# A hybrid encoder layer on one core: late low halves last in each product, a last row block in two tiles, and a new table of step times

## The chip, the cores and the metric

The kernel runs on one core of a Trainium2 chip. The core has five engines, each with a queue of its own that it works off in order: TensorE (PE; its weight loads are PEld), VectorE (DVE), ScalarE (ACT), GpSimd (POOL) and SyncE (SP), which here issues nearly all DMAs. The metric is the device time of one execution in microseconds (us).

## The reference

One layer of an encoder with two head groups side by side, for x of 1 × 4096 × 1024 in float32:

```python
def rmsnorm(x, g):
    y = xf * lax.rsqrt(jnp.mean(xf * xf, axis=-1, keepdims=True) + EPS)
    return y * g
...
#   x <- x + RMSNorm_post( W_out [ attn_out * silu(g_a) ; pool_out * silu(g_p) ] )
#   where [q | k | v | g_a | u_p | g_p] = RMSNorm_pre(x) @ W_in
#   - attention: windowed GQA (|i-j| <= 128) in blocks of 128 queries, 8 query and 2 key heads of 64,
#     a learned sink logit per head, T5 relative-position bias
#   - pooling: four channel groups, centred mean over windows 2/4/8/16 minus the token,
#     a linear map per group, a scale per channel
```

W_in has 1024 rows and 2304 columns, W_out is 1024 × 1024.

## The kernel before, in words

**Products.** TensorE works in fp16. Each float32 operand is a pair of a high and a low half (the low half is what the high one leaves), and each product is the sum of three terms: high by high, low weight by high x, high weight by low x. `high`/`low` (L2144, L2148), `x_hi`/`x_lo` (L336, L341) and lines 524 and 527 make the halves: ScalarE casts the high one, and VectorE or GpSimd subtracts it to get the low one. Before, the three terms alternate inside the loop over k, so that the third matmul of a product already reads the second low half.

**Phase one** (0 to about 484 us) computes the pooling half and the gates of RMSNorm_pre(x) @ W_in. The 4096 tokens are cut into eight macro-tiles m of 512. Macro-tile 0 uses plain products (`mm`, L975, `plain_ga`); the others use a scheme of seven products of half size (`product`, L1018) on sums of quarters of x and of the weights: A11, A12, S2, S1, S4, S3, A22. Meanwhile the weights are loaded (`w_load`, L395), multiplied by the norm's gain (`w_fold` on VectorE, L411; `w_fold_act` on ScalarE, L415), squared for their scale (`w_square`, L464; `norm_prod`, L468, sums the squares on TensorE), and written back to DRAM for phase two. The sums of squares of x's rows give row scales; `rs_row` (L306) stores the 512 of a macro-tile to DRAM in 4-byte pieces, and `rs_spread` (L310) loads them back as a broadcast `rb` for `y_scale` (L330). `x_turn` (L277) transposes the first x by DMA; `y_store` (L357) and `x_store` (L352, L354) keep x's halves in DRAM.

**Phase two** (about 484 us to the end) goes backward over 16 units u of two blocks of 128 rows, from block 31 to 0. For a block: `scores` (L1642), `logits` (L1659), `exps` (L1670), `probs` (L1713, high half) and `rests` (L1721, low half) make the probabilities `pn`, `turn` (L1733) transposes them by DMA, `values` (L2095) multiplies them with v, and `gate` (L2102) with the gate that `load_ga` (L2046) brings. `kv_product` (L1917) and `q_terms` (L1983) make k, v and q. The output product is again the scheme of seven (`product`, L2242), its sums are joined by `add` (L2284, tiles `mo`), and the norm follows: `square` (L2268), `mean` (L2294, L2299), `residual` (L2303), `store` (L2331). For the very last unit, 0, the output is four plain products per row block (`last_product`, L2214, with `last_square` L2229 and `last_gain` L2223), row block 1 in two tiles of 512 columns.

**Order.** Each step is put down by `due(t, fn, args)` with a time t from a plan written by hand; `moved` adds to that time what a table `later` (one per phase) holds for the step, sorts all steps by time, and the steps are issued in that order. Nothing is reordered after that: the numbers set only the order on each engine, not when something runs. SP's DMAs are in one queue too.

```python
out.append((t + later.get((*key, seen[key]), 0.0), n, fn, args))
```

## Time and profile before

| | |
|---|---|
| median of 3 executions | 1152.0 us (1149.72 to 1155.39) |
| the profiled execution | 1151.47 us |
| its span in the profile | 1149.6 us, mean granted clock 0.997 |
| TensorE busy | 1114.5 us (97%) |
| VectorE, ScalarE, GpSimd busy | 957.9 (83%), 723.3 (63%), 292.0 (25%) |
| moved by DMA | 262 MB, mean 228 GB/s |

In the rows of a timeline the first number is the start, the second the length (both us), then the engine, the line, what is written and what is read, a count, and in brackets the idle time before it and what ended that. A row of the waits names who waited for whom: us in total, times, the longest. SPq is SP's queue.

### The profile page before, as it was taken

Reading aid. Unit: us, or ns where it says so; the run is one execution under the profiler, and the core shown is the slowest. Engines: PE = TensorE matmul, PEld = TensorE weight load, DVE = VectorE, ACT = ScalarE, POOL = GpSimd, SP = SyncE. Lnnn points to the kernel's source line nnn. Section 1 sums busy time; section 2 is a strip of 40 time slices with the busy share of each in tenths; the row PEclk is TensorE's granted clock in tenths of the full one; section 3 lists DMA queues with packets and bytes.
Section 4 is the critical chain, followed back from the end, with each engine's and each line's share of the span. In section 5 each row is a group of like instructions: output and inputs, shape, how many; then the busy total and the mean of one; then the engine's idle time right before and its main releaser. Section 6 shows DMA issues by size and latency. Waiting matters only on the chain.

```text
span 1149.6 us, 28863 instructions
## 1 busy us (share of the span) xinstructions
PE 1114.5 (97%) x11532; PEld 816.6 (71%) x11532; DVE 957.9 (83%) x1973; ACT 723.3 (63%) x1622; POOL 292.0 (25%) x279
## 2 busy tenths in 40 slices
PE   6999999999999999999999999999999999999987
PEld 4547888888888888887566667667666666676443
DVE  6788787889869996867998898888888888988886
ACT  5766667666465635157766676676676666766672
POOL 1000000000000000001454554364454545544322
PEclk9999999999999999999999999999999999999999
DMA  9667878999879966999989898889989988889786
GB/s 250 169 230 247 229 214 303 265 266 275 268 231 279 262 238 215 346 266 256 251 193 214 210 211 208 211 187 239 208 186 227 197 198 223 211 206 200 141 186 199
DMA packets 328006, 262.02 MB, mean 228 GB/s; under 512 B 222608, under 2 KB 285712, under 8 KB 324416
## 3 DMA queue, kind: packets, MB, share of 16 engines
q1 hardware_dynamic: 323840, 245.50, 81.0%
q0 software_dynamic: 4032, 14.68, 5.2%
q8 instruction: 90, 1.47, 0.5%
q14 instruction: 44, 0.36, 0.1%
HBM read 130.87 MB, written 76.59 MB: 180 GB/s over the span
## 4 chain that ended last, share of the span: by engine, by line
PE 49%; DVE 26%; issue 9%; ACT 7%; DMA 6%; POOL 1%; SPq 0%; DVEq 0%; POOLq 0%; ACTq 0%
PE ch L1031 11%; PE aq_p L1983 7%; DVE p_all L1659 6%; DVE pn L1721 5%; PE ms L2242 5%; PE cl L1031 4%; PE m L2242 4%; PE a L981 4%; PE kp L1917 3%; PE pb L1031 3%; DVE ws L896 3%; DVE mo L2284 3%; PE pg L1092 2%; ACT pn L1713 2%; PE s L1642 1%
## 5 line engine op out<-in xcount | busy, mean ns | idle before, releaser
L1031 PEld LDWEIGHTS <-wa 128*128 128x128 f16 x3360 | 328.7, 98 | 38.9 <-issue 0.6
L1031 PE MATMUL ch<-xt,wa 128*128 128x256 f16 x1920 | 212.8, 273 | 0.3 <-ACT cbig L1043 0.3
L1670 ACT ACTIVATE p_all<-p_all,nm 128x385 f32<-128x385 f32 (+1 forms) x256 | 153.0, 599 | 59.0 <-DVE nm L1659 51.1
L1721 DVE SCALAR_TENSOR_TENSOR pn<-p_all,rd,pn 128x384 f16<-128x384 f32 (+1 forms) x256 | 159.0, 672 | 20.4 <-ACT pn L1713 18.6
L2242 PE MATMUL ms<-wa,ys 128*128 128x512 f16 x720 | 166.4, 381 | 3.9 <-DVE mo L2284 1.9
L1659 DVE CUSTOM_DVE_ANT_0 p_all<-s,ybig,nsink 128x385 f32<-128x385 f32 (+1 forms) x256 | 156.8, 664 | 7.9 <-PE s L1642 7.9
L1713 ACT ACTIVATE pn<-p_all,rd 128x384 f16<-128x384 f32 (+1 forms) x256 | 135.4, 596 | 8.9 <-issue 4.3
L2242 PE MATMUL m<-wa,y 128*128 128x512 f16 x540 | 124.2, 379 | 4.2 <-DVE mo L2284 3.3
L2242 PEld LDWEIGHTS <-ys 128*128 128x128 f16 x720 | 69.2, 98 | 81.7 <-issue 6.1
L1031 PE MATMUL cl<-xt,wa 128*128 128x256 f16 x960 | 106.3, 273 | 0.1
L2242 PEld LDWEIGHTS <-y 128*128 128x128 f16 x540 | 51.2, 98 | 65.4 <-issue 6.9
L249 POOL TENSOR_SCALAR ssq<-ssq 128x4 f32<-128x4 f32 (+1 forms) x11 | 3.7, 340 | 338.2 <-ACT jk L240 332.4
L2148 POOL TENSOR_TENSOR y<-yf,y 128x512 f16<-128x512 f32 x29 | 33.5, 1156 | 203.3 <-DMA wa<-w_scr 165.1
L341 DVE TENSOR_TENSOR xt<-ybig,xt 128x1024 f16<-128x1024 f32 x50 | 60.3, 1219 | 13.0 <-ACT xt L336 13.0
L2148 POOL TENSOR_TENSOR ys<-at,ys 128x512 f16<-128x512 f32 x28 | 36.5, 1305 | 132.1 <-ACT ys L2144 132.1
L2268 ACT ACTIVATE jkb<-mo 128x512 bf16<-128x512 f32 x42 | 26.3, 626 | 64.8 <-DVE mo L2284 64.8
L1917 PEld LDWEIGHTS <-raw 128*128 128x128 f16 x588 | 56.8, 98 | 14.1 <-issue 1.9
L1917 PE MATMUL kp<-xt,raw 128*128 128x256 f16 x540 | 65.4, 273 | 0.2 <-DVE at L2102 0.2
L2279 POOL TENSOR_TENSOR mo<-mo,ybig 128x512 f32<-128x512 f32 x39 | 52.4, 1343 | 45.2 <-ACT jkb L2268 45.0
L1642 PE MATMUL s<-k_all,q 64*32 64x288 f16 (+2 forms) x2856 | 60.0, 284 | 1.1 <-ACT k_all L1580 0.5
L1065 ACT ACTIVATE gp<-cbig,cg 128x256 f32<-128x256 f32 x42 | 19.0, 500 | 63.0 <-DVE cbig L1056 63.0
L336 ACT CAST xt<-ybig 128x1024 f16<-128x1024 f32 x50 | 51.6, 1040 | 7.2 <-PE cl L1031 4.4
(242 smaller groups left out, 2009.6 us busy)
## 6 DMA issues: line engine op xcount, KB each, us to landing
xn<-in_x SPq DMA_DIRECT2D x28, 512.0 KB
ybig<-in_xT SPq DMA_DIRECT2D x28, 512.0 KB
y_scr<-xt SPq DMA_DIRECT2D x14, 1024.0 KB
out<-mo SPq DMA_DIRECT2D x28, 512.0 KB
xt<-y_scr SPq DMA_DIRECT2D x26, 512.0 KB
xt<-in_x POOLq DMA_DIRECT2D x26, 512.0 KB, 5.0
xt<-x_scr SPq DMA_DIRECT2D x19, 512.0 KB
x_scr<-xt SPq DMA_DIRECT2D x9, 1024.0 KB
```

The source lines that it names most:

```text
L341: eng.tensor_tensor(out=o[:, w, 1], in0=y_view(i), in1=o[:, w, 0], op=ALU.subtract)
L1031: nc.tensor.matmul(acc[:, c], wa[:, q, wi, slot * HK + k, c * P : (c + 1) * P], x[:, xi, k, :], start=(fresh and n == 0), stop=(n > 3 * 2 ...
L1642: nc.tensor.matmul(s_bank[jj][r0 : r0 + nr, gg, lo:hi], q_t[u, half][a, qi, jj, tl + r0 : tl + r0 + nr], k_all[a, ki, k0 : k0 + hi - lo], ...
L1659: nc.vector.tensor_tensor_reduce(out=p_t[b, half][:, hh, :nk], in0=s_t[b, half][jj][:, gg, :nk], in1=bias[:, h, lo : lo + nk], scale=negc[ ...
L1670: nc.scalar.activation(p[:, hh, :nk], p[:, hh, :nk], AF.Exp, bias=nm_t[b, half][:, hh : hh + 1], scale=-1.0, accum_out=den_t[b, half][:, h ...
L1713: nc.scalar.activation(prob_view(b, half)[:, 0, i], p_t[b, half][:, i, :nk], AF.Copy, scale=rd_t[b, half][:, 0, i : i + 1],)
L1721: nc.vector.scalar_tensor_tensor(out=pn4[:, 1, i], in0=p_t[b, half][:, i, :nk], scalar=rd_t[b, half][:, 0, i : i + 1], in1=pn4[:, 0, i], o ...
L1917: nc.tensor.matmul(acc, wkv[:, slot, wi, k, :], x[:, xi, k, :], start=(onto is None and n == 0), stop=(n == 3 * HK - 1), skip_group_check= ...
L1983: nc.tensor.matmul(acc[:, jj], w[:, wi, jj, k, :], x[:, xi, k, :], start=(first and n == 0), stop=(last and n > 3 * 2 * HK - 3), skip_grou ...
L2148: eng.tensor_tensor(out=y[:, :, 1], in0=f(u), in1=y[:, :, 0], op=ALU.subtract)
L2242: nc.tensor.matmul(z_t[u, tag], y[:, k, yi, :], wo[o][:, wi, k // 2, k % 2, :], start=(n == 0 and acc is None), stop=(n == 3 * HK - 1), sk ...
L2279: eng.tensor_tensor(out=mo, in0=mo, in1=gpost[:, cs], op=ALU.mult)
```

## The change

It has three parts.

1. `term_order` puts the term with a late low half last: first, over all k, the high by high term and the one with the low half that is there early, then all matmuls with the other low half. It is used in `mm` (there the weight's low half is last), in both `product`s, `plain_ga`, `kv_product` and `last_product`. The number and shape of matmuls stay.
2. In unit 0, the second half of row block 1 is computed in two tiles of 256 columns, the second of them in a bank of the scores (`s_bank[1]`). `last_mean` adds what is known of the sum of squares ahead, `last_root` adds the rest, and the last 512 columns are finished by three engines: `residual` of 256 on VectorE, `last_rescale` of 256 on ScalarE and `last_sum` of these on GpSimd.
3. The two tables `later` get new entries and values. Three of them move the broadcasts `rs_spread` of macro-tiles 3, 5 and 6 (that of 4 gets a later time too).

```diff
+    def term_order(n, early=None):
+        a, b = ((0, 1), (1, 0)) if early else ((1, 0), (0, 1))
+        return [(k, w, x) for terms in (((0, 0), a), (b,)) for k in range(n) for w, x in terms]
...
-            for k in range(HK):
-                for wi, xi in ((0, 0), (1, 0), (0, 1)):
-                    for c in range(2):
+            for k, wi, xi in term_order(HK):
+                for c in range(2):
...
-            for k in range(KT):
-                for wi, xi in ((0, 0), (1, 0), (0, 1)):
+            for k, wi, xi in term_order(KT, "x"):
...
+            (x_turn, 0, 1): 0.4, ... (w_fold, 6, 1): -10.0, ... (rs_spread, 6, 1): 8.0, ...
+            (x_hi, 4, 'A11', 1): -10.0, ...
...
+    def last_mean():
+        ss = ss_t[0]
+        ms = rs_t["last"] = pb.tile([P, 1], F32, name="ms_last", tag="ms")
+        nc.vector.tensor_scalar(
+            out=ms, in0=ss[:, 2:3], scalar1=ss[:, 3:4], scalar2=epss, op0=ALU.add, op1=ALU.add
+        )
+
+    def last_root():
+        ms = pb.tile([P, 1], F32, name="ms_root", tag="ms")
+        nc.vector.tensor_tensor(out=ms, in0=ss_t[0][:, 4:5], in1=rs_t.pop("last"), op=ALU.add)
+        rs_t[0, 1] = pb.tile([P, 1], F32, name="rs_last", tag="rs")
+        nc.gpsimd.tensor_tensor(out=rs_t[0, 1], in0=ms, in1=mhalf, op=ALU.pow)
+
+    def last_rescale(cs):
+        mo = mo_t[0][1][:, cs]
+        nc.scalar.activation(mo, mo, AF.Copy, scale=rs_t[0, 1])
+
+    def last_sum(cs):
+        xr = xr_t[0][:, cs]
+        nc.gpsimd.tensor_tensor(out=xr, in0=mo_t[0][1][:, cs], in1=xr, op=ALU.add)
...
-    at_(36.8, last_product, 1, "22", O22, 1, True)
+    for part in QUARTERS:
+        at_(36.8, last_product, 1, "22", O22, 1, True, part)
...
-    at_(53.7, last_product, 1, "21", O12, 1, False)
+    at_(53.7, last_product, 1, "21", O12, 1, False, QUARTERS[0])
+    at_(55.0, last_product, 1, "21", O12, 1, False, QUARTERS[1])
...
+    at_(58.7, residual, 0, 1, LO)
+    at_(58.75, last_rescale, slice(768, D))
+    at_(58.8, last_sum, slice(768, D))
+    at_(59.4, residual, 0, 1, slice(512, 768))
...
+        ... (load_xr, 1, 1, 1): -0.8, (pool_in, 0, 0, 1): 1.5,
```

What that does to the queues, at three places. SP around 310 us, before; `rs_scr` is the store of the row scales of macro-tile 6, `rb6` their broadcast, `in_w_b` a weight of phase two:

```order
L306 DMA rs_scr_89<-ssq6_3302 128x4x1
L1107 DMA ga_scr_91<-sga4_1_1_3762 128x2x128 x2
L310 DMA rb6_3793<-rs_scr_89 128x512
L352 DMA x_scr_88<-xt_72 128x2048
L395 DMA raw_70<-in_w_b 128x1024
L1107 DMA ga_scr_91<-sga4_0_1_3854 128x2x128 x2
```

and in the changed kernel (its lines have other numbers):

```order
L311 DMA rs_scr_89<-ssq6_3302 128x4x1
L1109 DMA ga_scr_91<-sga4_1_1_3762 128x2x128 x2
L357 DMA x_scr_88<-xt_72 128x2048
L400 DMA raw_70<-in_w_b 128x1024
L1109 DMA ga_scr_91<-sga4_0_1_3852 128x2x128 x2
L315 DMA rb6_3884<-rs_scr_89 128x512
```

The broadcast has gone behind the store of x, the weight and two stores of gates. SP in the tail, before; `pn1_0` and `pn1_1` are the two transpositions of block 1, `ga_scr` the gate of block 1, `yp_scr` the pooled half (`pool_in`), `w_scr` the weights O12 of the last unit's products, `in_x` the x for the residual (`load_xr`):

```order
L1733 DMA_TRANSPOSE wa_73<-pn1_0_16154 128x24x128
L2046 DMA wa_73<-ga_scr_91 128x512
L2171 DMA yf0_0_16288<-yp_scr_90 128x512
L158 DMA wa_73<-w_scr_92 128x4x1024
L1733 DMA_TRANSPOSE wa_73<-pn1_1_16320 128x24x128
L2289 DMA raw_70<-in_x 128x1024 x2
```

and after:

```order
L2055 DMA wa_73<-ga_scr_91 128x512
L1743 DMA_TRANSPOSE wa_73<-pn1_0_16154 128x24x128
L158 DMA wa_73<-w_scr_92 128x4x1024
L2180 DMA yf0_0_16307<-yp_scr_90 128x512
L2324 DMA raw_70<-in_x 128x1024
L1743 DMA_TRANSPOSE wa_73<-pn1_1_16320 128x24x128
L2324 DMA raw_70<-in_x 128x1024
```

The gate's load stands ahead of the first transposition, the weights ahead of the pooled half, and one load of x ahead of the second transposition. VectorE in the tail, before; `pn2_0` are the low halves of block 2 (`rests`), `kq1_7` and `q0_0` belong to the queries of block 0, `mo2_0` is a row block of unit 2's output (`add`):

```order
L1721 SCALAR_TENSOR_TENSOR pn2_0_15874<-p_all_5964,rd2_0_15837,pn2_0_15874 128x384 x4
L2029 SCALAR_TENSOR_TENSOR kq1_7_14891<-aq7_p7_15706,kq1_7_14891 128x512
L2012 TENSOR_TENSOR q0_0_15906<-kq1_7_14891,q0_0_15906 128x512
L2284 TENSOR_TENSOR mo2_0_15555<-ms2_2_15883,mo2_0_15555 128x512
L1659 ISA p_all_5964,nm2_1_15998<-s0_5965,ybig_71,nsink_81,negc_80 128x385
```

and after:

```order
L1731 SCALAR_TENSOR_TENSOR pn2_0_15874<-p_all_5964,rd2_0_15837,pn2_0_15874 128x384 x3
L2038 SCALAR_TENSOR_TENSOR kq1_7_14891<-aq7_p7_15706,kq1_7_14891 128x512
L2319 TENSOR_TENSOR mo2_0_15555<-ms2_2_15883,mo2_0_15555 128x512
L1731 SCALAR_TENSOR_TENSOR pn2_0_15874<-p_all_5964,rd2_0_15837,pn2_0_15874 128x384
L2021 TENSOR_TENSOR q0_0_15906<-kq1_7_14891,q0_0_15906 128x512
L1669 ISA p_all_5964,nm2_1_15998<-s0_5965,ybig_71,nsink_81,negc_80 128x385
```

The addition to `mo2_0`, and with it the fourth of the `rests`, now stands between the two steps of the queries.

## The prediction

> **What bounds the kernel now.** I read the page first, then the waits of TensorE, then the timelines of the engines at each wait.

> ```profile
> span 1149.6 us, 28863 instructions
> PE 1114.5 (97%) x11532; PEld 816.6 (71%) x11532; DVE 957.9 (83%) x1973; ACT 723.3 (63%) x1622; POOL 292.0 (25%) x279
> ...
> PE aq L1983 <- DMA xt<-x_scr: 0.7, 1, 0.7
> ```

> TensorE is busy for 97% of the span, so nothing done off it counts unless TensorE waits for it. Its waits are short ones, such as the 0.7 us for x in this list, and none that the change can reach is over 2.2 us (the rows further down). So the sum goes wait by wait. The windows say which engine sets the pace in each stage:

> ```profile
> 484.00:560.00 76.00, 73.58 (x894) 58.90 (x893) 59.17 (x163) 45.87 (x121) 9.31 (x8) 1.00 1.00 263
> 1045.00:1108.00 63.00, 58.45 (x652) 32.69 (x650) 56.08 (x136) 41.80 (x108) 21.90 (x19) 1.00 0.71 152
> 1115.63:1119.04 3.41, 3.41 (x20) 1.71 (x16) 2.57 (x10) 3.11 (x12) 0.00 (x0) 0.50 1.11 366
> ```

> After the length come PE, PEld, DVE, ACT and POOL, then granted clock, DMA share, GB/s. At 484, where the second phase begins, the DMA share is 1.00. In the tail (1045 to 1108) VectorE is busy 56.08 of 63 us and TensorE waits for it. For 3.41 us from 1115.63 the granted clock is 0.50.

> **The change part by part.** The waits that it can reach, on TensorE:

> ```profile
> 24.69 2.84 PE L968 MATMUL gp<-xt,wa 128*128 128x128 f16 x48 [0.78 <-DMA xt<-cbig]
> 49.92 5.14 PE L981 MATMUL a<-xt,wa 128*128 128x512 f16 x23 [0.93 <-DVE wa L527]
> 55.71 0.38 PE L468 MATMUL n<-wsq,ones 128*128 128x2 f32 x2 [0.66 <-ACT wj L464]
> 342.15 0.38 PE L468 MATMUL n<-wsq,ones 128*128 128x1 f32 x2 [2.12 <-ACT wj L464]
> 551.61 2.33 PE L2242 MATMUL ms<-wa,ys 128*128 128x512 f16 x10 [0.56 <-POOL ys L2148]
> 557.09 2.78 PE L1983 MATMUL aq_p<-xt 128*128 128x256 f16 x24 [0.40 <-DVE mo L2284]
> 605.33 2.75 PE L2242 MATMUL m<-wa,y 128*128 128x512 f16 x12 [0.93 <-DVE mo L2284]
> 1078.52 5.34 PE L2242 MATMUL ms<-wa,ys 128*128 128x512 f16 x24 [1.40 <-DVE mo L2284]
> 1109.39 2.75 PE L2242 MATMUL ms<-wa,ys 128*128 128x512 f16 x12
> 1112.07 1.17 PE L2095 MATMUL o<-wa,vv 128*64 128x256 f16 x18
> 1115.25 1.81 PE L2095 MATMUL o<-wa,vv 128*64 128x256 f16 x18 [2.01 <-DMA wa<-pn]
> 1116.99 3.76 PE L2242 MATMUL ms<-wa,ys 128*128 128x512 f16 x12
> ```

> *1, start.* The third transposition of x is late by 0.78. One of the two weight loads that stood ahead of it now goes ahead of the first, so that SP gets to it sooner by that load's issue, and 0.5 MB less is in front of it.

> ```profile
> 12.86 0.57 SPq L395 DMA_DIRECT2D raw<-in_w_a  x1
> 13.52 3.52 SPq L277 DMA_TRANSPOSE xt<-cbig  x1
> 17.09 0.58 SPq L395 DMA_DIRECT2D raw<-in_w_a  x1
> 17.77 6.43 SPq L277 DMA_TRANSPOSE xt<-cbig  x2
> ```

> By 12.86 to 13.52 that is 0.66, plus its bytes; I take −0.7. Ends: −0.8 (all of the wait) and +1.5 (the load in front of the first transposition delays it: 0.5 MB at the 366 GB/s of the last window above is 1.4).

> *2, 47 to 57.* In `mm` the weight's low half is now used after 16 of 24 matmuls. The 23 of the row above took 5.14, so 16 are 3.6 us, more than the 0.93: this wait goes, covered by the high terms. The 0.66 is for `w_square` on ScalarE behind `w_fold(6)` on VectorE, which now stands some 10 us earlier in the table. −1.6; ends −0.9 (the second stays) and −1.6.

> *3, 342.* The cause is on SP, 30 us ahead. The broadcast load (L310) waits for the store of the row scales to land, and `in_w_b` is queued behind it:

> ```profile
> 307.40 0.59 SPq L306 DMA_DIRECT2D rs_scr<-ssq  x1
> 310.28 1.50 SPq L1107 DMA_DIRECT2D ga_scr<-sga  x2
> 320.96 0.33 SPq L310 DMA_DIRECT2D rb<-rs_scr  x1
> 321.82 0.43 SPq L395 DMA_DIRECT2D raw<-in_w_b  x1
> 330.45 1.28 ACT L415 ACTIVATE raw<-raw,g_pre 128x128 f32<-128x128 f32 x4 [3.41 <-DMA raw<-in_w_b]
> 344.19 2.35 DVE L330 TENSOR_TENSOR ybig<-ybig,rb 128x1024 f32<-128x1024 f32 x2
> ```

> With the broadcast behind it, `in_w_b` can go at about 312; at the 8.6 us that it took (321.82 to 330.45) it is there at 321, before ScalarE first asks (330.45 − 3.41 = 327.0). ScalarE is then 3.4 ahead at the square for which TensorE waited 2.12: −2.1. Ends: −2.1 and 0 (its buffer isn't free before 321.8). The broadcast, after 322, is not needed before 344.19, so its later place costs nothing. The two others that move (of macro-tiles 3 to 5) wait for no engine's work either, by the same distance: nothing.

> *4, 545 to 606.* 0.56 + 0.40 + 0.93 = 1.89. An `add` goes ahead of the last `rests`, and two low halves change place on POOL and VectorE. Each fills a wait with work that stands on the same engine anyway, and what is late next is the next VectorE step. Less than half: −0.8, ends 0 and −1.9.

> *5, tail, VectorE.* `add` of `mo2_0` now stands in a wait for ScalarE:

> ```profile
> 1076.36 1.51 DVE L2012 TENSOR_TENSOR q<-kq,q 128x512 f16<-128x512 f32 x1 [0.69 <-ACT q L2008]
> 1077.79 0.68 DVE L2284 TENSOR_TENSOR mo<-ms,mo 128x512 f32<-128x512 f32 x1
> ```

> 0.68 of work fits 0.69 of waiting, but it is put ahead of a `rests`, for which ScalarE isn't waited. −0.5; ends +0.7 (it merely delays the transposition behind) and −1.4, the whole wait of TensorE at 1078.52.

> *6, the last full transposition.* TensorE waits 2.01 for `pn1_1`, which SP issued at 1106.89, 8.36 before it was used:

> ```profile
> SPq L2171 <- DVE at L2180: 3.8, 1, 3.8
> ...
> 1102.81 0.32 SPq L2171 DMA_DIRECT2D yf<-yp_scr  x1
> 1103.23 0.54 SPq L158 DMA_DIRECT2D wa<-w_scr  x1
> 1106.89 4.91 SPq L1733 DMA_TRANSPOSE wa<-pn  x1
> ```

> `w_scr` (1 MB) was held on SP behind `yf`, which waited 3.8 us for VectorE. At the 152 to 366 GB/s of the windows above it moves for 2.9 to 6.9 us, until 1106 or 1110, and so may run into the transposition. It now goes ahead of `yf`, right behind the transposition of `pn1_0`, 2 to 4 us sooner; against that, 0.5 MB of x is put between, and the gate's load ahead of `pn1_0` must wait for VectorE's `gate`. The transposition's own length I estimate at 5 to 6 us (SP alone is held 4.91), so unobstructed it lands near 1112.5; TensorE is ready at 1113.24 (1112.07 + 1.17). −1.3; ends −2.0 and +1.0 (0.5 MB more in front).

> *7, the clock.* The halved clock costs 3.76 − 2.75 and 1.81 − 1.17 = 1.65, and it starts after an idle of 2.01; the 2.12 at 342 cost no clock, since it lies across a boundary of the 3.41 us steps. A wait cut to under 1 us should not do it: −1.65; ends 0 and −1.65. [...]

> *8, end.* After the last matmul:

> ```profile
> 1143.11 0.60 ACT L2229 ACTIVATE jkz<-z 128x512 bf16<-128x512 f32 x1 [1.90 <-PE z L2214]
> 1143.83 0.27 DVE L2294 TENSOR_SCALAR ms<-ss,epss 128x1 f32<-128x1 f32 x1 [1.24 <-ACT jkz L2229]
> 1144.82 1.41 DVE L2303 SCALAR_TENSOR_TENSOR raw<-xt,rs,raw 128x512 f32<-128x512 f32 x2
> ```

> The square is half as wide (I take −0.15 of 0.60), the mean's step is one addition (−0.1), VectorE adds 768 instead of 1024 columns (a quarter of 1.41, −0.3) with 256 on ScalarE and POOL beside it; 48 matmuls of 256 for 24 of 512 are at most +0.15. −0.4; ends +0.3 (POOL ends last) and −0.7.

> The order of terms elsewhere has no wait to remove and adds no instruction: 0.

> Sum: −0.7 − 1.6 − 2.1 − 0.8 − 0.5 − 1.3 − 1.65 − 0.4 = −9.05. The profiled execution took 1151.47 (span 1149.6 and 1.9 around it), 0.5 under the median 1152.0. 1152.0 − 9.05 = 1143.

> **The rivals.** A: the tail's transposition is as late as before, since 1.5 MB and not 1.25 stand ahead of it; terms 6 and 7 fall away, 1143 + 2.95 = 1146. Speaks for it: more bytes in one queue. Against: they start sooner. B: the wait shrinks, the clock halves nevertheless: 1144.6. C: the phase boundary takes back terms 1 to 3. There the DMA share is 1.00 and TensorE waits 0.7 for x from DRAM; if bytes and not TensorE set the end of phase one, 4.4 are lost: 1147.4. Against it: these DMAs are stores and loads that follow TensorE's products, and so move with them. A and C together: 1150.3. D, slower: ScalarE's cast of `A11` for macro-tile 4 is put some 7 us earlier, ahead of three copies that free accumulators, and writes where an earlier half was stored from:

> ```profile
> 221.57 0.50 SPq L357 DMA_DIRECT2D y_scr<-xt  x1
> ...
> 232.43 1.05 ACT L1043 COPY cbig<-ch 128x512 f32<-128x512 f32 x2
> 239.77 1.03 ACT L336 CAST xt<-ybig 128x1024 f16<-128x1024 f32 x1
> ```

> If that 1 MB store lands after 232.4, when the cast's turn comes, ScalarE stands, then TensorE, one for one, and 1.7 more for a halved clock. The decision against 1152 falls at a landing near 240; at 245, 12.6 + 1.7 − 9.05 gives 1157. The store has 10.9 us from its issue; `in_w_b`, half its size, took 8.6 and the row scales 13.5 (307.40 to 320.9), so it isn't excluded, but hardly 24 us.

> **How the numbers follow.** The forecast 0.45 (its own range 1140 to 1146), A 0.17, B 0.10, C 0.17, A with C 0.06, D 0.05. The range 1139 to 1150.5 takes in all but D and the far ends. A change under 0.5% (5.8 us) can't be told from none here: faster means under 1146.2, which holds the forecast, most of B and half of A: 0.60; slower, over 1157.8, D and what I don't see, 0.06; the same 0.34.

> **What would show it.** Right: no wait at 50, 55 and 340 for `wa` and `wj`; `in_w_b` issued about 9 us ahead of the broadcast of macro-tile 6; the wait for `wa<-pn` before the last `values` of block 1 under 1 us and a clock of 1.00 from there to the end; span after the last matmul near 6.2 instead of 6.6. Wrong: a longer wait at 484 to 500 for `x_scr`, which is C; a wait of ScalarE before its cast near 232, which is D; new waits of TensorE for VectorE in 545 to 606 as long as those gone.

## The result, and the profile after

The changed kernel takes 1143.7 us (median of 10 executions, 1142.14 to 1146.1), the kernel before 1150.45 on the same chip (10 executions, 1147.45 to 1155.39): a ratio of 0.9944, 95% interval 0.9931 to 0.9956. The forecast was 1143.0. The two profiled executions are 8.8 us apart (1142.67 against 1151.47), 2 us more than the medians, whose gain is 6.75. So the forecast gain of 9.05 is met by the two profiles, and only in part by the medians: the forecast started from 1152.0, the median of three executions, and from 1150.45 the same sum would have given 1141.4.

The head of the page, then rows of TensorE's timeline that stand where the prediction showed waits (line numbers are the changed kernel's):

```profile
span 1140.9 us, 28920 instructions
PE 1110.8 (97%) x11556; PEld 816.5 (72%) x11556; DVE 961.1 (84%) x1975; ACT 725.0 (64%) x1625; POOL 292.5 (26%) x280
```

```profile
16.89 5.90 PE L973 MATMUL gp<-xt,wa 128*128 128x128 f16 x96
23.90 2.84 PE L973 MATMUL gp<-xt,wa 128*128 128x128 f16 x48 [1.11 <-DMA xt<-cbig]
...
47.50 5.34 PE L985 MATMUL a<-xt,wa 128*128 128x512 f16 x24
52.68 0.28 PE L473 MATMUL n<-wsq,ones 128*128 128x2 f32 x2
...
336.94 0.28 PE L473 MATMUL n<-wsq,ones 128*128 128x1 f32 x2
...
597.95 2.76 PE L2277 MATMUL m<-wa,y 128*128 128x512 f16 x12
...
1058.99 0.93 PE L1652 MATMUL s<-k_all,q 64*32 64x288 f16 x48 [1.22 <-DVE k_all L1898]
...
1070.70 5.36 PE L2277 MATMUL ms<-wa,ys 128*128 128x512 f16 x24
...
1078.72 2.76 PE L2277 MATMUL m<-wa,y 128*128 128x512 f16 x12 [1.58 <-ACT y L2153]
1082.84 2.75 PE L2277 MATMUL ms<-wa,ys 128*128 128x512 f16 x12 [1.35 <-DVE mo L2319]
...
1107.78 1.17 PE L2104 MATMUL o<-wa,vv 128*64 128x256 f16 x18 [0.59 <-DMA wa<-pn]
```

The waits of 0.93 and 0.66 near 50, of 2.12 at 342 and of 0.93 at 605 are gone; that for `pn` fell from 2.01 to 0.59, and 18 matmuls after it take 1.17, not 1.81: full clock. New are 1.22 for `k_all` at 1058.99 and 1.58 for `y` at 1078.72, and the wait for `mo` at 1082.84 is 1.35 where it was 0.48.

Since the products come in the same order, the start of the same matmul can be compared in both profiles. Its lead (after less before, us) and how it changes:

| matmul, before → after | lead | change | step, predicted |
|---|---|---|---|
| 46.01 → 45.27 | −0.74 | −0.74 | 1: −0.7 |
| 55.71 → 52.68 | −3.03 | −2.29 | 2: −1.6 |
| 342.15 → 336.94 | −5.21 | −2.18 | 3: −2.1 |
| 544.91 → 539.23 | −5.68 | −0.47 | none |
| 605.33 → 597.95 | −7.38 | −1.70 | 4: −0.8 |
| 1000.05 → 992.41 | −7.64 | −0.26 | none |
| 1108.78 → 1102.72 | −6.06 | +1.58 | 5: −0.5 |
| 1115.25 → 1107.78 | −7.47 | −1.41 | 6: −1.3 |
| last one's end, 1143.00 → 1134.43 | −8.57 | −1.10 | 7: −1.65 |
| span, 1149.6 → 1140.9 | −8.7 | −0.1 | 8: −0.4 |

The sum agrees with the forecast, but two terms (2 and 4) are larger than predicted, two (7 and 8) smaller, and one (5) has the other sign. SP's queue and ScalarE, ahead of step 3:

```profile
305.72 0.68 SPq L311 DMA_DIRECT2D rs_scr<-ssq  x1
...
310.55 2.20 SPq L400 DMA_DIRECT2D raw<-in_w_b  x1
...
320.23 0.33 SPq L315 DMA_DIRECT2D rb<-rs_scr  x1
...
323.79 1.28 ACT L420 ACTIVATE raw<-raw,g_pre 128x128 f32<-128x128 f32 x4
```

The weight is issued 9.7 us ahead of the broadcast, and ScalarE has no wait for it (3.41 before).

### The profile page after: what moved, and what is told of

Same layout as the page of the kernel before. It is cut to its first block, busy times and chain, and to the rows that moved or that the text cites. A ratio compares the mean times of both kernels' runs of the same rounds, so it can differ in the third digit from the quotient of the medians.

```text
span 1140.9 us, 28920 instructions
## 1 busy us (share of the span) xinstructions
PE 1110.8 (97%) x11556; PEld 816.5 (72%) x11556; DVE 961.1 (84%) x1975; ACT 725.0 (64%) x1625; POOL 292.5 (26%) x280
## 5 line engine op out<-in xcount | busy, mean ns | idle before, releaser
L1731 DVE SCALAR_TENSOR_TENSOR pn<-p_all,rd,pn 128x384 f16<-128x384 f32 (+1 forms) x256 | 161.5, 681 | 20.1 <-ACT pn L1723 17.4
L2303 ACT ACTIVATE jkb<-mo 128x512 bf16<-128x512 f32 x42 | 26.3, 626 | 63.1 <-DVE mo L2319 63.1
L1652 PEld LDWEIGHTS <-q 64*32 64x32 f16 (+1 forms) x2856 | 38.4, 92 | 27.1 <-issue 24.6
```

What stands on the lines that cost most here:

```text
L1652: nc.tensor.matmul(s_bank[jj][r0 : r0 + nr, gg, lo:hi], q_t[u, half][a, qi, jj, tl + r0 : tl + r0 + nr], k_all[a, ki, k0 : k0 + hi - lo], ...
L1731: nc.vector.scalar_tensor_tensor(out=pn4[:, 1, i], in0=p_t[b, half][:, i, :nk], scalar=rd_t[b, half][:, 0, i : i + 1], in1=pn4[:, 0, i], o ...
L2303: nc.scalar.activation(junk, src, AF.Square, scale=2.0**-5, accum_out=ss_t[u][:, 2 * i + c : 2 * i + c + 1])
```

## The experiments

They ran on three other chips, where the kernel before takes 1146.3 to 1146.7 us. Each ratio is against executions of it on the same chip.

### The three parts one by one

**`terms`**: the kernel before with part 1 alone.

```
+ for k, wi, xi in term_order(KT, "x"): ...     tables and last row as before
```

> Only the new order of terms; the old tables and the old last row. Theory (each wait is worth what its row says, part by part): the wait of 0.93 for the weight's low half at 50 goes, and the 0.56 for POOL's low half at 552; next to nothing else, since the other waits are for high halves, additions and transpositions: 1 to 1.5 us faster, ratio about 0.999. Rival (the order of terms carries the change, the table only follows it): 4 us or more.

Measured: 1147.16, ratio 1.0004 (0.9992 to 1.0016): nothing. Its timeline:

```profile
48.67 5.35 PE L985 MATMUL a<-xt,wa 128*128 128x512 f16 x24 [0.26 <-ACT wa L529]
55.78 0.38 PE L473 MATMUL n<-wsq,ones 128*128 128x2 f32 x2 [1.76 <-ACT wj L469]
```

The wait of 0.93 for the low half is gone, and the next, for `wj`, grew from 0.66 to 1.76: ScalarE didn't come sooner, so what TensorE had won it waited for 7 us later. The same happened at 551 to 557, where 0.56 and 0.40 became one wait of 0.93.

**`table_one`**: the new times of phase one alone.

```
  moved(..., later={... (w_fold, 6, 1): -10.0, ... (rs_spread, 6, 1): 8.0, ...})     phase one only
```

> Only the new table of phase one; old order of terms, old last row, old table of phase two. Theory: the waits at 24 (about 0.8), 48 to 56 (0.3 to 1.5, since the low half of the weight is still used third) and 342 (2.1) go or shrink, and TensorE reaches phase two 3.5 to 4.5 us earlier, which lasts to the end: ratio 0.996 to 0.997. Rival (the phase boundary, where the DMA share is 1.00, takes it back): the lead is there at 480 and gone at 500.

Measured: 1142.85, ratio 0.9971 (0.9961 to 0.998). With the old order of terms, the timeline lists no wait at the first product (its row is 0.29 longer than in the changed kernel), and none at the two steps behind:

```profile
47.04 5.63 PE L981 MATMUL a<-xt,wa 128*128 128x512 f16 x24
52.51 0.28 PE L468 MATMUL n<-wsq,ones 128*128 128x2 f32 x2
...
336.12 0.28 PE L468 MATMUL n<-wsq,ones 128*128 128x1 f32 x2
```

So step 2 belongs to the table and hardly to the order of terms; which of its entries carries it was not run singly. Against the profile of the kernel before, the lead is 6.50 at 480 and 6.41 at 500: it was kept across the phase boundary, and rival C is out. Against the mean of the five profiles from these chips that have the old table of phase one (`terms`, `split`, `table_two`, `ot3`, `rb6`), it is 3.0 at 55.71 and 4.0 at 480, so that steps 1 and 2 are three quarters of it.

**`table_two`**: the new times of phase two alone.

```
  moved(..., later={... (sum2, 2, 1): -0.8, ... (load_xr, 1, 1, 1): -0.8, ...})     phase two only
```

> Only the new table of phase two. Theory: 1 to 1.5 us at 556 to 606 (additions ahead of rests); in the tail a loss of about 1 us where VectorE meets POOL (sum2 of unit 2 earlier), then 1.4 us less waiting for the last full transposition and 1.6 us less for the halved clock: 3 us, ratio 0.997 to 0.998. Rival: the tail's gain is there only since TensorE came earlier from phase one; then 1 us or nothing.

Measured: 1146.38, ratio 0.9997 (0.9986 to 1.0009). Its profile has the new waits for `k_all` (1.22, at 1063.94) and for `y` (1.59): they come from these times. Over the kernel before, the lead grows by 0.94 from 544.91 to 605.33 and falls by 1.29 at the scores (−2.68 to −1.39), so the loss there takes back what the new times won.

**`split`**: the last row in two tiles with three engines alone.

```
+ for part in QUARTERS: at_(36.8, last_product, 1, "22", O22, 1, True, part)
+ at_(58.75, last_rescale, ...); at_(58.8, last_sum, ...)
```

> Only the last row in two tiles, finished by three engines; old order of terms, old tables. Theory: from the last matmul to the end of the last addition 0.1 us less (square and mean 0.3 less, the additions on VectorE 0.2 more beside POOL), 0.1 more on TensorE: no difference, ratio 1.000 within its interval. Rival, as I forecast: 0.4 us less.

Measured: 1146.51, ratio 1.0002 (0.9988 to 1.0016). From the last matmul to the end it took 6.48, 0.09 less than before, as the theory had it. The profiled execution, 1152.64, was the slowest of its 12: SP stood 6 us in its queue, the transposition behind was late, and a halved clock followed (18 matmuls took 2.01, the 18 ahead of the wait 1.17), in code that this edit doesn't touch:

```profile
526.71 0.36 SPq L2046 DMA_DIRECT2D wa<-ga_scr  x1
533.02 0.53 SPq L158 DMA_DIRECT2D wa<-w_scr  x1
533.65 6.25 SPq L1734 DMA_TRANSPOSE wa<-pn  x1
```

```profile
543.43 2.01 PE L2095 MATMUL o<-wa,vv 128*64 128x256 f16 x18 [3.59 <-DMA wa<-pn]
```

**`after_again`**: the changed kernel itself on another chip.

> The changed kernel unaltered, on the chip of these runs, where the kernel before is faster than on the first one (1146.7 against 1150.45). Theory (the parts add up, and the first chip's larger gain came from waits of the kernel before that vary from execution to execution): ratio near the product of the four parts, 0.997. Rival (the parts need each other): 0.9944 as on the first chip.

Measured: 1142.37, ratio 0.9967 (0.9955 to 0.998). The product of the four ratios above is 0.9974, so the parts add up within the intervals, and the table of phase one carries the whole.

### What the tail lost

**`no_sum2`**: the changed kernel without one entry, that of unit 2's `sum2` on VectorE.

```diff
-        (sum2, 2, 1): -0.8, (gain11, 2, 0, 1): -0.8, (probs, 2, 0, 0, 1): -0.8,
+        (gain11, 2, 0, 1): -0.8, (probs, 2, 0, 0, 1): -0.8,
```

> The changed kernel without one entry: sum2 of unit 2 on VectorE stands again behind the copy of k, not ahead of it. Theory (ahead of it, it lets GpSimd start its low half 1 us sooner, beside VectorE's copy and rests in float16, which then took 1.13 and 1.63 for 0.29 and 0.61 us): these go back to 0.3 and 0.6, and the tail's scores no longer wait 1.2 for the copy: 1 to 1.8 us faster than the changed kernel. Rival (VectorE is as late anyhow, since GpSimd's work comes later and meets other steps): within 0.5 us of it.

Measured: 1140.25 (1139.89 to 1140.86), ratio 0.9951 (0.9937 to 0.9964), 2.1 us less than `after_again` on the same chip with no overlap of their executions. It beats both kernels. VectorE and GpSimd at this place, before:

```profile
1064.84 0.29 DVE L1888 COPY k_all<-k_all 128x512 f16<-128x512 f16 x1
1065.05 0.61 DVE L1721 SCALAR_TENSOR_TENSOR pn<-p_all,rd,pn 128x384 f16<-128x384 f32 x1
...
1067.59 2.08 POOL L2148 TENSOR_TENSOR ys<-at,ys 128x512 f16<-128x512 f32 x1 [4.88 <-ACT ys L2144]
```

in the changed kernel:

```profile
1056.22 0.68 DVE L2192 TENSOR_TENSOR at<-s,at 128x512 f32<-128x512 f32 x1
...
1057.81 1.13 DVE L1898 COPY k_all<-k_all 128x512 f16<-128x512 f16 x1
1058.86 1.63 DVE L1731 SCALAR_TENSOR_TENSOR pn<-p_all,rd,pn 128x384 f16<-128x384 f32 x1
...
1057.64 1.15 POOL L2157 TENSOR_TENSOR ys<-at,ys 128x512 f16<-128x512 f32 x1 [2.56 <-ACT ys L2153]
1058.75 1.32 POOL L2189 TENSOR_TENSOR at<-at,yf 128x512 f32<-128x512 f32 x1
```

and without the entry:

```profile
1056.47 0.29 DVE L1898 COPY k_all<-k_all 128x512 f16<-128x512 f16 x1
1056.68 0.61 DVE L1731 SCALAR_TENSOR_TENSOR pn<-p_all,rd,pn 128x384 f16<-128x384 f32 x1
...
1059.22 2.08 POOL L2157 TENSOR_TENSOR ys<-at,ys 128x512 f16<-128x512 f32 x1 [4.88 <-ACT ys L2153]
```

The earlier sum (the first row of the changed kernel) lets GpSimd start its low half at 1057.64 instead of behind VectorE's steps, and so beside them. The copy, 0.29 otherwise, takes 1.13 and ends 0.15 after GpSimd's instruction, and the `rests`, 0.61 otherwise, take 1.63 and end 0.42 after GpSimd's next one. Why they take longer beside GpSimd no run shows; without the entry both are at 0.29 and 0.61 again. So VectorE lost 1.9 us (0.84 + 1.02) ahead of the scores.

### Single entries of the tables

**`ot3`**: the kernel before with the load of a weight of phase two moved past others.

```diff
+        (load_wo, 7, 1): -6.0,
```

> The kernel before with one entry of the new table of phase two: the load of the weights OT3 stands ahead of the transposition of pn30_0 on SP, not ahead of that of pn30_1, where SP was held 4.6 to 5.9 us by an earlier DMA. Theory (that hold makes the transposition of pn30_1 late in some executions, 3.6 us of waiting and a halved clock in one profile): pn30_1 is issued by 529, no wait for it; the median up to 1 us lower, the slowest executions 3 to 5 us lower. Rival: only that one profile had it; no difference.

Measured: 1147.41, ratio 1.0003 (0.9991 to 1.0014): nothing. The transposition is issued at 530.62, not by 529, and TensorE doesn't wait for it; of the profiles with the old order only that of `split` has this wait. The slowest of 11 executions took 1148.77, against 1152.43 among 21 of the kernel before, but `rb6`, which lacks the entry, doesn't go over 1148.3 either: an effect on the slowest executions is not shown.

**`rb6`**: the kernel before with the broadcast of macro-tile 6 later.

```diff
+            (rs_spread, 6, 1): 8.0,
```

> The kernel before with one entry of the new table of phase one: the broadcast of macro-tile 6 behind the load of in_w_b and two stores. Theory: in_w_b is issued at about 312 and ScalarE no longer waits 1.9 to 3.4 for it; TensorE gains what it waited at 340 in that execution, 0 to 2.1 us: ratio 0.998 to 1.000. Rival (the wait moves on to the next load behind, x of macro-tile 6): ratio 1.000 and a new wait of TensorE by 360.

Measured: 1146.61, ratio 0.9997 (0.9985 to 1.0008): nothing. The edit does what step 3 says, `in_w_b` is issued at 312.72 and ScalarE has no wait. But in none of the four profiles with the old order from these chips (`terms`, `table_two`, `split`, `ot3`) did TensorE wait there: the broadcast was issued 1.0 to 2.4 us sooner, and ScalarE had the weight at 327.3 to 328.3 and not at 330.45, early enough:

```profile
327.35 1.28 ACT L415 ACTIVATE raw<-raw,g_pre 128x128 f32<-128x128 f32 x4 [2.43 <-DMA raw<-in_w_b]
```

### What the gain needs

**`tables_only`**: the kernel before with both tables, without the entry of `sum2`; old order of terms, old last row.

```
  parts 1 and 2 undone; of part 3 all but (sum2, 2, 1)
```

> The kernel before with the new times of both phases, without the earlier sum of unit 2; the order of terms and the last row are as before. Theory: the new order of terms and the split of the last row are worth nothing by themselves, and the sum of unit 2 was a loss, so all of the gain is in the times: 0.995 of the kernel before, as the changed kernel without that sum (0.9951), 1140.3 us. Rival: the terms with a late low half matter once the waits for the weights' high half are gone by the times, at 50, 55 and 545 to 606: then some of 0.9 + 0.7 + 1.9 us comes back, 1 to 3 us more, 0.996 to 0.998.

Measured: 1141.34, ratio 0.995 (0.9936 to 0.9963). **`finish_one`**: `no_sum2` with the last 512 columns finished by VectorE alone.

```diff
-    at_(58.75, last_rescale, slice(768, D))
-    at_(58.8, last_sum, slice(768, D))
-    at_(59.4, residual, 0, 1, slice(512, 768))
+    at_(59.4, residual, 0, 1, HI)
```

> The changed kernel without the earlier sum of unit 2 (as in the run before that left this entry out, 0.9951 of the kernel before, 1140.25 us), and the last 512 columns of the last row are finished by VectorE alone (one rescaling and addition of 256 and then one of 512 columns) instead of by three engines. Theory: the additions of VectorE beside ScalarE and POOL take 1.61 us in the changed kernel where two halves of 512 took 1.41 alone, so the help costs as much as it saves: last matmul to end of span within 0.2 us of 6.47, ratio 0.995. Rival: the three engines save what a third addition costs alone (256 of 1024 columns, a quarter of 1.41): 0.3 us more from the last matmul to the end, ratio 0.9954; a difference this small shows in the profile's end alone and hardly in the times.

Measured: 1140.65, ratio 0.9945 (0.9932 to 0.9957). By the times these two and `no_sum2` are the same; the 0.7 us between the first two, on one chip, isn't resolved by five executions each. The end of the profiles shows more; the last addition of the changed kernel, its companion on GpSimd, and the same addition in `finish_one` (the edit leaves two of 512 columns):

```profile
1135.91 1.61 DVE L2338 SCALAR_TENSOR_TENSOR raw<-xt,rs_last,raw 128x512 f32<-128x512 f32 x2 [0.39 <-POOL rs_last L2260]
...
1136.50 0.74 POOL L2268 TENSOR_TENSOR raw<-xt,raw 128x256 f32<-128x256 f32 x1 [0.62 <-ACT xt L2264]
```

```profile
1133.45 1.41 DVE L2338 SCALAR_TENSOR_TENSOR raw<-xt,rs_last,raw 128x512 f32<-128x512 f32 x2 [0.39 <-POOL rs_last L2260]
```

VectorE needs 1.61 for 768 columns beside GpSimd and 1.41 for 1024 alone. From the last matmul's end to the end of the span it is 6.24 in `finish_one` and 6.47 with three engines: the help costs 0.2.

**`old_queue`**: `no_sum2` with the tail's queue of before.

```diff
-        (turn, 2, 1, 1): -0.8, (product, 1, 's2', 5, 1, 1): 0.8, (turn, 1, 0, 1): 1.5,
+        (turn, 2, 1, 1): -0.8, (product, 1, 's2', 5, 1, 1): 0.8,
-        (square, 1, 1, 0, 1): 0.8, (load_xr, 1, 1, 1): -0.8, (pool_in, 0, 0, 1): 1.5,
+        (square, 1, 1, 0, 1): 0.8,
```

> The changed kernel without the earlier sum of unit 2, and with three times of the tail taken back: the load of the pool's weights goes behind the load of yf again, and the load of x and the transposition of pn1_0 stand as before. Theory: the wait of TensorE for the transposition of pn1_1 is 1.5 to 2.3 us again instead of 0.6, and in some executions a 3.41 us window of halved clock follows (1.65): 1.0 to 3.0 us more than 1140.25, ratio 0.996 to 0.998. Rival: the transposition is early enough in this queue too, as in the run of the first phase's times alone, where it was waited for some 0.4 us: no difference, 0.995.

Measured: 1142.17 (1140.11 to 1142.66), ratio 0.9954 (0.9941 to 0.9966). This settles little. The wait for `pn1_1` is 0.93, between the two expectations; 2.5 us of its profiled execution are a wait for `q` at 529, which `tables_only` has too (2.2) and `no_sum2` and `finish_one` haven't, and which no entry here explains: SP was held 10.09 and 9.78 us at a transposition there, against 6.6 to 7.0. More is in the profiles taken together:

```profile
1112.23 1.17 PE L2096 MATMUL o<-wa,vv 128*64 128x256 f16 x18 [2.26 <-DMA wa<-pn]
```

```profile
1107.70 1.17 PE L2104 MATMUL o<-wa,vv 128*64 128x256 f16 x18 [0.93 <-DMA wa<-pn]
```

These are `terms` and `old_queue`. With `yf` ahead of `w_scr` the wait was 2.01 (before), 2.26, 1.49 (`ot3`), 0.93, 0.38 (`split`) and under 0.15 (`table_one`, `rb6`). With `w_scr` ahead it was 0.59 (after), 0.68 (`after_again`), 0.43 (`table_two`, `no_sum2`), 0.32 (`finish_one`) and 0.16 (`tables_only`). So the new queue takes away the large ones; on the mean of 7 and of 6 profiles that is about 0.6 us, not 1.4. But in `split` and `rb6` a half clock had begun some 11 us ahead of it (22 matmuls from 1106.66 and 1100.67 took 6.61, against 4.92 in `tables_only`), TensorE came 1.5 us later for that, and so waited less. The time from the issue of the transposition to its use is freer of that: 8.36, 8.61, 7.84, 7.27, 8.09, 6.47 (`table_one`) and at most 7.68 (`rb6`) in the old queue, 6.94, 7.02, 6.78, 6.77, 6.66 and 6.51 in the new one. That is 1.0 us less on the mean, and the two ranges overlap.

### The clock

**`clock`**: a probe. Bursts of matmuls, and between them chains of VectorE that TensorE waits for.

```
for j in range(72):
    for i in range(44 + j * 5 % 17): matmul(acc, w, x)        # 512 columns, fp16
    t = acc * xs; for _ in range(j % 6): t = t * xs           # VectorE
    x = t * 0 + 0.01                                          # the next burst needs it
```

> A probe: no layer is computed, the output is a copy of x. 72 bursts of 44 to 60 matmuls of 512 columns on TensorE; after each, VectorE goes through a chain of 1 to 6 copies for which the next burst waits, so TensorE is idle for about 0.5 to 4 us between bursts of 10 to 13 us. [...]

Measured in windows of 3.41 us, counted from the changes of the clock in this one execution: of 272 windows at full clock, 40 were followed by half clock. The highest busy share of TensorE among these 40 was 0.401, the lowest among the other 232 was 0.439. The two windows with these shares, each with the one after it (length, then busy PE, PEld, DVE and POOL, clock, DMA share, GB/s):

```profile
733.94:737.35 3.41, 1.37 (x7) 0.50 (x6) 1.94 (x3) 0.00 (x0) 1.00 0.00 0
737.35:740.76 3.41, 0.71 (x2) 0.26 (x2) 2.51 (x5) 0.00 (x0) 0.50 0.00 0
1099.17:1102.58 3.41, 1.50 (x7) 0.59 (x6) 1.81 (x3) 0.00 (x0) 1.00 0.00 0
1102.58:1105.99 3.41, 0.58 (x3) 0.29 (x3) 2.64 (x5) 0.00 (x0) 1.00 0.00 0
```

By length of the idle, half clock followed 1.1 to 1.84 us in 0 of 24, 2.56 in 6 of 12, 3.3 in 10 of 12, and 4.0 to 4.75 in 23 of 23. Two of the 2.56:

```profile
226.85 12.89 PE L82 MATMUL acc<-x,w 128*128 128x512 f16 x59 [2.56 <-DVE x L86]
```

```profile
317.00 3.53 PE L82 MATMUL acc<-x,w 128*128 128x512 f16 x9 [2.56 <-DVE x L86]
```

The first lies across the boundary of two windows at 225.36: TensorE was busy for 2.35 of the 3.42 us ahead of it and for 1.92 of the 3.41 behind it, and the clock stayed at 1.00. The second lies in the window from 314.10 (busy for 0.85 of 3.41, a share of 0.25), and half clock follows (9 matmuls in 3.53). So in this execution two idles of one length went different ways, and half clock followed windows that weren't wholly idle, here with a share of up to 0.40, in the kernel before with one of 0.41.

## Why the prediction was right, and where not

*Step 1*, right in size and in its main cause. The matmul starts when the third transposition lands, at 23.90 instead of 24.69:

```profile
17.61 6.03 SPq L282 DMA_TRANSPOSE xt<-cbig  x2
```

In the seven profiles with this entry it started at 23.61 to 24.10 (mean 23.85), in the six without it at 24.17 to 24.79 (mean 24.56), so the 0.7 is a gain of the change. The issue gave less of it than the 0.66 that the prediction took: the transposition was issued at 17.61 instead of 17.77, and the rest is a quicker landing. The wait itself grew, 0.78 to 1.11, because TensorE was ready sooner: the clock became full at 17.67 instead of 19.95, so that 96 matmuls took 5.90 and not 6.96. That time differs between executions (17.3 to 20.5 in the thirteen profiles), and it gained nothing, since the landing set the start.

*Step 2*, under-sized (−2.29 for −1.6; a wait of 0.26 at 48.60, which it left out, goes too) and credited wrongly. The prediction let the order of terms cover the 0.93; `terms` shows that it doesn't cover the step behind, and `table_one` and `tables_only` that the table does it without that order.

*Step 3*, right in mechanism and size for the profiled execution. What it left out is that a DMA's landing differs between executions: ScalarE had the weight at 330.45 in this one, and at 327.3 to 328.3 in four on the other chips, where the wait wasn't there. That is 2.1 of the 2.8 us by which the gain of the medians is larger on the first chip (6.75) than for `after_again` (3.91); that it is the cause there was not traced in more than one execution.

*Step 4*, under-sized: −1.70 of 1.89, where "what is late next is the next VectorE step" had halved it. It is the table's as well: `tables_only`, with the old order of terms, has −1.69 there, `terms` 0.

*Step 5*, the term that failed. The 1.40 at 1078.52 did vanish (the lead went from −6.34 to −7.82). But the prediction counted only the `add`, and the table also moves `sum2`, which it passed over. And it counted a wait of TensorE, although its windows had shown VectorE setting the pace from 1045 on. VectorE's `logits` behind the two moved steps, before:

```profile
1068.57 0.67 DVE L1659 CUSTOM_DVE_ANT_0 p_all<-s,ybig,nsink 128x385 f32<-128x385 f32 x1
...
1078.39 0.67 DVE L1659 CUSTOM_DVE_ANT_0 p_all<-s,ybig,nsink 128x385 f32<-128x385 f32 x1
```

and after:

```profile
1062.80 0.67 DVE L1669 CUSTOM_DVE_ANT_0 p_all<-s,ybig,nsink 128x385 f32<-128x385 f32 x1
...
1072.34 0.67 DVE L1669 CUSTOM_DVE_ANT_0 p_all<-s,ybig,nsink 128x385 f32<-128x385 f32 x1
```

VectorE's lead was −7.64 at the `logits` of 1058.09. It is −5.77 at the first of these, so the copy of k and the `rests` beside GpSimd cost 1.9; and −6.05 at the second, so the `add` won 0.28, not 0.5. Together that is the +1.58 of the table. TensorE has this lead wherever it waits for VectorE's chain: for its waits of 1.58 (by way of ScalarE), 1.35, 0.83 and 0.43, at 1084.77, 1088.88, 1101.14 and 1108.78 before, it is −6.05, −6.04, −6.06 and −6.06, whatever it won between (−7.48 at 1103.44, where the wait of 1.25 for a low half is gone). In `no_sum2` the lead is −8.37 at 1040, and the same four are −8.65, −8.64, −8.66 and −8.66: without the loss, the same 0.28. The order of terms thus moves waits in the tail and ends none: its 0 in the sum was right.

*Step 6*, right in this pair (−1.41), with a mean nearer 1.0 over the profiles. The transposition isn't issued earlier (5.18 and 5.17 us ahead of the block's first `values`); it lands sooner, 6.94 after its issue instead of 8.36. The estimate of 5 to 6 us for its own length was short: no profile shows it used sooner than 6.47 after its issue. Rival A didn't occur.

*Step 7*, right, and rival B didn't occur. The window of 3.41 us that holds the wait, before and after (counted from the changes of the clock in each trace, 1115.63 and 17.67):

```profile
1112.22:1115.63 3.41, 1.40 (x26) 1.24 (x24) 2.79 (x7) 2.32 (x6) 0.28 (x1) 1.00 1.20 210
```

```profile
1106.52:1109.93 3.41, 2.41 (x35) 1.78 (x30) 3.16 (x8) 2.16 (x7) 0.72 (x1) 1.00 0.93 287
```

TensorE was busy in it for 1.40 of 3.41 (0.41, followed by a clock of 0.50), and now for 2.41 (0.71, followed by 1.00). The 1.65 came as −1.10, mainly since a wait of 0.41 for VectorE stands behind it.

*Step 8*, over-sized: of −0.4 there was −0.1, since VectorE beside GpSimd takes 1.61 and not the 1.06 that three quarters of 1.41 would be. Without the help the end is 0.33 shorter: 6.57 before, 6.24 in `finish_one`.

D didn't occur, TensorE shows no wait of that kind in macro-tile 4. So the number came out through errors that cancel: −1.6 too little in steps 2 and 4, +2.1 in step 5, +0.55 and +0.3 in 7 and 8, and −0.7 between the steps, where short waits elsewhere shrank. That the total fits is luck as far as these go. On another chip, without the wait of step 3, the medians gained 3.91, less than half of the forecast. And the work that carries the gain is one part of three: with the times alone, less one entry, the same 0.995 is reached.

## What to carry to other kernels

A step that is moved is costed on every engine that it sets free: an earlier sum on VectorE started GpSimd beside VectorE's next steps, and that cost VectorE 1.9 us. Where one engine sets the pace of a stage, follow its chain from anchor to anchor; what another engine gains between two anchors it gives back at the second. A wait that hangs on a DMA's landing in one profile is read as a sample, and several executions tell what it is worth.

## What was not expected of the hardware

The kernel's windows don't part at these shares. In `rb6` waits of 0.50 and 1.25 in one window left 0.49, and half clock followed (in `split` the 6.61 came behind the same two waits); in `tables_only` a window of 0.46 was followed by full clock:

```profile
1097.34:1100.76 3.42, 1.66 (x16) 0.73 (x16) 3.28 (x6) 1.46 (x5) 1.26 (x1) 1.00 0.16 61
1100.76:1104.17 3.41, 3.41 (x9) 1.24 (x10) 3.41 (x7) 3.02 (x7) 0.31 (x1) 0.50 0.74 220
...
1077.66:1081.07 3.41, 1.58 (x7) 0.62 (x8) 3.41 (x6) 1.60 (x4) 1.22 (x1) 1.00 0.13 49
1081.07:1084.48 3.41, 2.93 (x15) 1.23 (x13) 3.41 (x9) 1.65 (x5) 0.00 (x0) 1.00 0.93 173
```

What else counts was not tested. Two short waits in one window stood ahead of half clock in `rb6`, as the one of 2.01 did in the kernel before.

Of the probe's 50 windows at half clock, 39 were followed by full clock, with TensorE busy in each for a share of 0.82 or more; behind the other 11, with 0.70 or less, the half clock stayed for another 3.41 us. Shares between were not met.

The same transposition at 515 us in phase two held SP for between 6.4 and 10.1 us in the profiles of the changed kernel and its variants.
